# An encoder's token mixer: ones from DRAM, q and k read from a held PSUM bank, and a margin for handing TensorE work of head pairs over

## The chip, the cores and the metric

The kernel runs on one core of a Trainium2 chip. The metric is the device time of one execution in microseconds (us). The engines are TensorE (PE, matmuls; its weight loads are shown as PEld), VectorE (DVE), ScalarE (ACT), GpSimd (POOL) and SyncE (SP, which here only issues DMAs).

## What is computed

Two layers over 256 tokens of width 1024 in float32: half a gated feed-forward step, a mixer of a recurrent branch and an attention branch, and another half feed-forward step. The change touches the attention branch.

```python
h = rms_norm(x, g_mix[l]); z = h @ w_in[l]
q, k, v = three 1024-column parts of z, as 16 heads of 64
f_logit = 16 columns of z + b_forget[l]
qn, kn = rms_norm(q, g_q), rms_norm(k, g_k)            # per head
cum = cumsum(log_sigmoid(f_logit), over time)
s = qn @ kn.T / 8 + cum[query] - cum[key], causal      # per head
o = softmax(s) @ v
y_lru = (gelu(z_lg) * rg_lru(conv(z_lx))) @ w_lru_out[l]
m = sigmoid(gate_A) * y_lru + sigmoid(gate_B) * (o @ w_attn_out[l])
x = x + m @ w_o[l]
```

## The kernel before

**Main matmuls.** Every float32 weight chunk (two row groups of 128 by 512 columns) is loaded by a DMA into `raw`, split into a high part `whi` (ACT, line 325) and a rest `wlo` (DVE, line 334), and used by `visit` in three matmuls per 128 rows (lines 365 to 367). A block of 512 output columns takes four chunks and, for each of the two groups of 128 tokens (`tok`), 24 matmuls into one PSUM bank. There are two x banks, two y banks and four z banks. In the mixer the blocks come in this order: recurrent input, recurrent gate, v, then q and k of heads 0 to 7 (`hf` 0), q and k of heads 8 to 15 (`hf` 1), four gate blocks, and the three output projections.

**Side work.** What is done with a bank is written as generators (chains). The planner `Sched` runs while the program is written, not on the chip. It keeps a modelled time per engine; after every main matmul group `hook` steps the chains that `may` be stepped by that model. So it fixes the order in which each engine's instructions stand, and each engine then works its queue in that order, waiting where data is missing. A chain yields either a modelled time and an engine or another chain that it waits for. `need` forces a chain to its end, whatever the model says.

```python
def may(self, c):
    if c.wait is not None:
        if not c.wait.over:
            return False
        c.ready = self.now
    if c.eng == "p":
        return c.ready <= self.now
```

**q and k.** `ev_qk` scales a bank by `rs(tok)` into `nat` and squares it into `sq` (ACT). `qk_chain` sums the squares per head (line 883), takes the power -1/2 on POOL (line 887), multiplies `nat` by it (line 890), transposes it on PE into a z bank (`quad`, line 449) and scales it into `qk[w, hf]` (w is 0 for q and 1 for k). In that tile 32 partitions hold rows that pick one head's bias (POOL copies from `ident`, line 910) and 32 hold `cum` (`bias_chain`, lines 309 and 312).

**Head pairs.** `pair_chain(j, prev)` handles heads 2j and 2j+1: scores on PE (line 943), mask and minimum on DVE (959), exponentials on ACT (968), reciprocal (973) and scaling, six transposes (449), copies `pt`, and products with V into a y bank that two pairs share (1001). Before the products it yields `prev`, the pair ahead of it. `att_chain` adds the pairs in order, with at most `NLIVE` = 2 at work, and adds `bias_chain` ahead of pairs 0 and 4. Behind the gate blocks `S.need(att)` waits for all pairs. `ot_chain` splits a y bank when its two pairs are done.

Of the kernel before, what the change touches and what calls it, by code (L numbers as in the profile page):

```python
# [15 lines left out]
P = 128  # L16
# [22 lines left out]
SLACK = 2.5  # L39
IDLE = 1.6  # L40
HSTEP = 3.0
LAT = 0.3
LSIG = 2.6
POW = 2.3
# [3 lines left out]


class Chain:  # L50
    def __init__(self, gen, ready, eng, bg):
        self.gen, self.ready, self.eng, self.bg = gen, ready, eng, bg
        self.over = False
        self.wait = None

# [8 lines left out]
class Sched:  # L64
# [25 lines left out]
    def busy(self, eng):  # L90
        return self.t[eng] - self.now

    def add(self, gen, ready=0.0, eng="p", bg=False):
        c = Chain(gen, ready, eng, bg)
        self.chains.append(c)
        return c

# [16 lines left out]
# [3 lines that stand above are left out]
                return False  # L117
            c.ready = self.now
        if c.eng == "p":
            return c.ready <= self.now  # L120
        if c.bg and self.busy(c.eng) > SLACK:
            return False
        return c.ready <= max(self.now, self.t[c.eng]) + 0.05
# [38 lines left out]
def hybrid_encoder_kernel(  # L162
# [15 lines left out]
    tmp_p = ctx.enter_context(tc.tile_pool(name="tmp", bufs=NTMP))  # L178
    att_p = ctx.enter_context(tc.tile_pool(name="att", bufs=NLIVE))
    sm_p = ctx.enter_context(tc.tile_pool(name="sm", bufs=2))  # L180
    ps_x = ctx.enter_context(tc.tile_pool(name="ps_x", bufs=2, space=bass.MemoryType.PSUM))
    ps_y = ctx.enter_context(tc.tile_pool(name="ps_y", bufs=2, space=bass.MemoryType.PSUM))
    ps_z = ctx.enter_context(tc.tile_pool(name="ps_z", bufs=4, space=bass.MemoryType.PSUM))
# [7 lines left out]
    def new(pool, shape, tag, dt=F32):  # L191
        return pool.tile(shape, dt, tag=tag, name=nm(tag))

    nat_ring, z_ring, y_ring, tmp_ring = [], [], [], []

    def new_nat(n=512):
        r = S.claim(nat_ring, NNAT)
        return new(nat_p, [P, n], "nat"), r
# [23 lines left out]
    def free(s):  # L222
        free_slots.append(s[1])
        s[0] = None
# [4 lines left out]
    def bc(ap, n):  # L229

        return ap.unsqueeze(2).to_broadcast([ap.shape[0], ap.shape[1], n])
# [153 lines left out]
    def block(lhs, evac, pool, ncol=512, norm=None, mixed=False):  # L385

        nk = 1024 // ncol
        n = KD // nk
        i0 = take(n)
        accs = {}  # L390
        order = [(tok, i) for tok in range(NT) for i in range(n)]
        if mixed:
            order = [(tok, i) for i in range(n) for tok in range(NT)]
        for tok, i in order:
            if i == 0:
                a, r = pool()
                accs[tok] = a[:, :ncol], r
            acc, r = accs[tok]

            def fin():  # L400
                evac(tok, acc)
                r.free = True

            if norm is not None:
                norm.before(tok, i * nk)
            visit(i0 + i, acc, lhs, i * nk, tok, i == 0, i == n - 1, fin if i == n - 1 else None)
# [139 lines left out]
    def rs(tok):  # L546
        return rstd[:, tok:tok + 1]

    def xbank():
        r = Rec()  # L550
        return bank(ps_x, "x"), r


# [69 lines left out]


    fw = {}

    def load_fw(l):
        r, rr = new_tmp([P, KD, H])
# [34 lines left out]
    def mix(l, nrm):  # L663
# [213 lines left out]
        qk = {}  # L877
        qk_c = {0: [], 1: []}

        def qk_chain(w, hf, tok, nat, sq, dep):  # L880
            yield dep, "d"
            rq = sm_p.tile([P, 8], F32, tag="rq", name=nm("rq"), bufs=4)
            nc.vector.tensor_reduce(out=rq, in_=sq[0].rearrange("p (h d) -> p h d", d=DH), axis=AX.X, op=ALU.add)
            sq[1].free = True
            nc.vector.tensor_scalar(out=rq, in0=rq, scalar1=1.0 / DH, scalar2=EPS, op0=ALU.mult, op1=ALU.add)
            d = S.use("d", dve_c(512) + 0.1)
            nc.gpsimd.tensor_tensor(out=rq, in0=rq, in1=mhalf, op=ALU.pow)
            yield d + POW, "d"
            n3 = nat[0].rearrange("p (h d) -> p h d", d=DH)
            nc.vector.tensor_tensor(out=n3, in0=n3, in1=bc(rq, DH), op=ALU.mult)  # L890
            yield S.use("d", dve_c(512)), "p"
            ps, rz = zbank()
            quad(nat[0], ps)
            nat[1].free = True
            gcol = gqm[:, l:l + 1] if w == 0 else col(R_GK)
            for e in range(2):
                yield S.now, "d"
                b = slice(e * DH, e * DH + DH)
                scale_any(qk[w, hf][0][b, e, :, tok * P:(tok + 1) * P], k4(ps)[b], gcol[b], 512)
            rz.free = True  # L900

        def quarters(w):

            return [(e, slice(r, r + 32), slice(r ^ 32, (r ^ 32) + 32)) for e, r in ((0, 64 + 32 * w), (1, 32 * w))]

        def new_qk(w, hf):
            t = qk[w, hf] = slot([P, 2, KD // 2, T])
            for e, one, _ in quarters(w):
                c0 = one.start + hf * 8 + e
                nc.gpsimd.tensor_copy(t[0][one, e], bc(ident[one, c0:c0 + 7:2], T))  # L910

        def bias_chain(hf):
            for w in range(2):
                for e, _, acc in quarters(w):
                    yield S.now, "d"
                    n = KD // 2
                    copy_any(qk[w, hf][0][acc, e], cum[acc].unsqueeze(1).to_broadcast([32, n, T]), n * T, S.now, True)


        OT = {}  # L920
# [88 lines left out]
        def att_chain():  # L1009
            while not tables[0]:  # L1010
                if lru.over:
                    break
                yield S.now + 0.5, "p"
            yield late[0]
            live, c = [], None
            for j in range(H // 2):
                for c_ in qk_c[j // 4]:
                    yield c_
                if j % 4 == 0:
                    yield S.add(bias_chain(j // 4), S.now, "d")  # L1020
                if len(live) >= NLIVE:
                    yield live.pop(0)
                c = S.add(pair_chain(j, c), S.now, "p", True)
                live.append(c)
                yield S.now + HSTEP, "p"
            for c in live:
                yield c

        att = None
        for hf in range(2):  # L1030
            for w in range(2):
                new_qk(w, hf)

                def ev_qk(tok, acc):
                    nat = new_nat()
                    scale_any(nat[0], acc, rs(tok), 512)
                    sq = new_tmp()
                    nc.scalar.activation(sq[0], acc, AF.Square, scale=rs(tok))
                    dep = S.use("a", act_c(512, 1))
                    c = S.add(qk_chain(w, hf, tok, nat, sq, dep), dep, "d")  # L1040
                    nat[1].user = sq[1].user = c
                    S.step(c)
                    qk_c[hf].append(c)
                block(lhs, ev_qk, xbank)
            if hf == 0:
                att = S.add(att_chain(), S.now, "p", True)

# [93 lines left out]
    def rows_chain():  # L1141
# [4 lines left out]
        for l in range(L):  # L1146
# [6 lines left out]
            S.use("d", 0.3)  # L1153
            rz.free = True
        free(rows_s)
        yield from load_fw(0)

    def program():
# [75 lines left out]
```

## Time and profile before

| | |
|---|---|
| median of 3 runs (lowest to highest) | 1287.18 us (1287.1 to 1287.46) |
| profiled execution: its time, its span | 1288.31 us, 1286.6 us |
| busy share: PE, PEld, DVE, ACT, POOL | 98%, 81%, 64%, 61%, 7% |
| granted TensorE clock, mean | 0.999 of full speed |
| chain that ended last, by engine | PE 90%, DVE 6%, ACT 2%, DMA 2%, issue 1% |

The span is the time from the first to the last instruction in the profile; what lies around it is 1.7 us. A matmul's record lasts longer than the step to the next one, since matmuls are pipelined; so busy shares of PE are upper bounds, and the step from start to start is the pace. The first layer's mixer lies between about 184 and 450 us, the second layer's between about 820 and 1085 us, with the same pattern.

### The profile page before, as it was taken

The numbers are of one execution on the slowest core, as the hardware profiler recorded it, in microseconds if no ns is written. First come the engines' busy times: TensorE is split into PE (matmuls) and PEld (weight loads), VectorE is DVE, ScalarE is ACT, GpSimd is POOL, SyncE is SP. The second block draws the span as 40 slices with busy tenths as digits, with TensorE's granted clock in tenths as the row PEclk, the third lists the DMA queues.
The fourth block names the chain that finished last, engine by engine and source line by source line (L and its number), as shares of the span: only waits on it lengthen the run. The fifth ranks groups of instructions, "written<-read, shape, count | busy, mean of one in ns | idle before, by whom it ended". The sixth has DMA issues, their size and how long they took to land.

```text
span 1286.6 us, 16397 instructions
## 1 busy us (share of the span) xinstructions
PE 1266.1 (98%) x6033; PEld 1047.3 (81%) x6033; DVE 824.5 (64%) x1151; ACT 780.6 (61%) x1064; POOL 84.9 (7%) x85
## 2 busy tenths in 40 slices
PE   8999999999999999999999999999999999999998
PEld 6888888887778888888888888888877788888887
DVE  5655558799765666555475555678987557655553
ACT  6655556777855456555566555558768455555553
POOL 4000001005100000000000000000250000000000
PEclk9999999999999999999999999999999999999999
DMA  8967667365346657666677776664644465687762
GB/s 265 241 203 206 208 167 237 106 197 153 119 134 202 195 184 215 208 207 209 180 209 218 212 213 213 155 213 126 185 145 141 144 200 159 202 235 208 214 196 80
DMA packets 175488, 241.44 MB, mean 188 GB/s; under 512 B 56440, under 2 KB 68912, under 8 KB 175408
## 3 DMA queue, kind: packets, MB, share of 16 engines
q1 hardware_dynamic: 174560, 240.29, 62.5%
q8 instruction: 47, 0.77, 0.2%
q14 instruction: 33, 0.27, 0.1%
q0 software_dynamic: 832, 0.11, 0.1%
q10 hardware_dynamic: 16, 0.00, 0.0%
HBM read 227.78 MB, written 1.05 MB: 178 GB/s over the span
## 4 chain that ended last, share of the span: by engine, by line
PE 90%; DVE 6%; ACT 2%; DMA 2%; issue 1%; SPq 0%; ACTq 0%; DVEq 0%
PE x L365 13%; PE x L366 13%; PE x L367 13%; PE z L366 12%; PE z L367 12%; PE z L365 12%; PE y L367 3%; PE y L365 3%; PE y L366 3%; PE z L449 2%; DVE wlo L334 2%; PE z L943 2%; PE z L771 1%; DMA nat<-tmp 1%; PE y L1001 1%
## 5 line engine op out<-in xcount | busy, mean ns | idle before, releaser
L334 DVE TENSOR_TENSOR wlo<-raw,whi 128x1024 fp32r<-128x1024 f32 x424 | 514.1, 1227 | 226.0 <-ACT whi L325 218.7
L325 ACT CAST whi<-raw 128x1024 fp32r<-128x1024 f32 x424 | 442.1, 1050 | 248.3 <-PE z L367 126.0
L365 PE MATMUL x<-whi,s 128*128 128x512 f32 x832 | 337.2, 405 | 5.3 <-ACT s L470 3.5
L366 PE MATMUL x<-wlo,s 128*128 128x512 f32 x832 | 325.1, 391 | 1.8 <-DVE wlo L334 1.1
L367 PE MATMUL x<-whi,s 128*128 128x512 f32 x832 | 325.2, 391 | 0.1
L365 PE MATMUL z<-whi,s 128*128 128x512 f32 (+1 forms) x752 | 279.7, 372 | 0.0
L367 PE MATMUL z<-whi,s 128*128 128x512 f32 (+1 forms) x752 | 279.4, 371 | 0.0
L366 PE MATMUL z<-wlo,s 128*128 128x512 f32 (+1 forms) x752 | 279.3, 371 | 0.0
L365 PEld LDWEIGHTS x<-whi,s 128*128 128x128 f32 x832 | 156.5, 188 | 39.0 <-ACT s L470 5.8
L367 PEld LDWEIGHTS x<-whi,s 128*128 128x128 f32 x832 | 156.3, 188 | 34.5 <-DVE s L472 1.2
L366 PEld LDWEIGHTS x<-wlo,s 128*128 128x128 f32 x832 | 156.7, 188 | 32.3 <-DVE wlo L334 1.9
L365 PEld LDWEIGHTS z<-whi,s 128*128 128x128 f32 x752 | 141.7, 188 | 24.4
L366 PEld LDWEIGHTS z<-wlo,s 128*128 128x128 f32 x752 | 141.8, 189 | 24.3
L367 PEld LDWEIGHTS z<-whi,s 128*128 128x128 f32 x752 | 141.7, 188 | 24.3
L312 ACT COPY tmp<-nat 128x1024 uint16<-128x1024 uint16 (+1 forms) x76 | 84.1, 1133 | 68.6 <-DMA nat<-tmp 60.7
L603 DVE SCALAR_TENSOR_TENSOR nat<-z,rstd,nat 128x512 f32<-128x512 f32 (+1 forms) x48 | 33.9, 706 | 61.0 <-PE z L367 61.0
L365 PE MATMUL y<-whi,s 128*128 128x512 f32 x176 | 69.1, 393 | 0.0
L367 PE MATMUL y<-whi,s 128*128 128x512 f32 x176 | 68.6, 390 | 0.0
L366 PE MATMUL y<-wlo,s 128*128 128x512 f32 x176 | 68.6, 390 | 0.0
L502 POOL TENSOR_TENSOR rstd<-msum,mhalf 128x1 f32<-128x1 f32 x12 | 11.8, 985 | 805.8 <-DVE msum L500 805.8
L472 DVE TENSOR_TENSOR s<-tmp,s 128x512 fp32r<-128x512 f32 (+1 forms) x72 | 47.2, 656 | 22.6 <-ACT s L470 22.6
L598 ACT ACTIVATE nat<-z,rstd 128x512 f32<-128x512 f32 (+1 forms) x46 | 30.0, 651 | 48.9 <-PE z L367 48.9
(154 smaller groups left out, 919.2 us busy)
## 6 DMA issues: line engine op xcount, KB each, us to landing
raw<-in_w_up_dram SPq DMA_DIRECT2D x176, 512.0 KB, 4.6
raw<-in_w_in_dram SPq DMA_DIRECT2D x112, 512.0 KB, 4.3
raw<-in_w_down_dram SPq DMA_DIRECT2D x88, 512.0 KB, 4.5
raw<-in_w_lru_out_dram SPq DMA_DIRECT2D x16, 512.0 KB, 3.6
raw<-in_w_attn_out_dram SPq DMA_DIRECT2D x16, 512.0 KB, 4.8
raw<-in_w_o_dram SPq DMA_DIRECT2D x16, 512.0 KB, 4.6
tmp<-in_b_gate_dram SPq DMA_DIRECT2D x8, 256.0 KB, 4.3
xn<-in_x_dram SPq DMA_DIRECT2D x4, 256.0 KB, 5.0
```

Source lines behind the costliest of these rows:

```text
L312: nc.scalar.copy(out_, in_)
L325: nc.scalar.copy(hi, raws[i])
L334: nc.vector.tensor_tensor(out=lo, in0=raws.pop(i), in1=f32(hi), op=ALU.subtract)
L365: nc.tensor.matmul(acc, lhsT=lhs(0, k0 + kk)[:, ts], rhs=hi[:, kk, :], start=st, stop=False)
L366: nc.tensor.matmul(acc, lhsT=lhs(0, k0 + kk)[:, ts], rhs=lo[:, kk, :], start=False, stop=False)
L367: nc.tensor.matmul(acc, lhsT=lhs(1, k0 + kk)[:, ts], rhs=hi[:, kk, :], start=False, stop=sp)
L449: nc.tensor.transpose(dst_ps[:, j * P:(j + 1) * P], src[:, j * P:(j + 1) * P], ident)
L472: nc.vector.tensor_tensor(out=lo, in0=t, in1=f32(hi), op=ALU.subtract)
L598: nc.scalar.activation(s[tok][0], acc, AF.Silu, scale=rs(tok))
L603: nc.vector.scalar_tensor_tensor(out=h, in0=acc, scalar=rs(tok), in1=h, op0=ALU.mult, op1=ALU.mult)
L771: nc.tensor.matmul(ps[:, g, :], lhsT=wax[0][:, g, n, :], rhs=xr[0][:, n, :], start=True, stop=True)
L943: nc.tensor.matmul(p_[:, qb * P:qb * P + nk], lhsT=qk[0, hf][0][:, e, jj, qb * P:(qb + 1) * P], rhs=qk[1, hf][0][:, e, jj, :nk], start=Tru ...
```

## The change

The tiles with the rows of ones are made once by ACT (`ones_chain`), written to DRAM, and read from there by DMAs on the POOL queue where POOL copied before. `ev_qk` no longer scales into `nat`: the bank is held (`held`, `r.free`) until `qk_chain` multiplies it by `rs(tok)` and by the per-head factor in one DVE instruction that reads PSUM; k of `hf` 0 goes to the y banks. `Chain` gets a field `late`, 1.5 for pairs and for q and k, by which PE work of such a chain is handed over later than the model has it ready. `bias_chain` ends with a wait for its last copy.

```diff
-    def __init__(self, gen, ready, eng, bg):
-        self.gen, self.ready, self.eng, self.bg = gen, ready, eng, bg
+    def __init__(self, gen, ready, eng, bg, late):
+        self.gen, self.ready, self.eng, self.bg, self.late = gen, ready, eng, bg, late
...
         if c.eng == "p":
-            return c.ready <= self.now
+            return c.ready + c.late <= self.now
...
             def fin():
-                evac(tok, acc)
-                r.free = True
+                held[0] = r
+                r.free = evac(tok, acc) is None
...
     def xbank():
-        r = Rec()
+        r = S.claim(x_ring, 2)
...
+    ones_d = [dram.tile([P, 2, KD // 2, T], F32, name=f"ones_d{hf}") for hf in range(2)]
+    def ones_chain():
+        for hf in range(2):
+            t = slot([P, 2, KD // 2, T])
+            for w in range(2):
+                for e, one, _ in quarters(w):
+                    c0 = one.start + hf * 8 + e
+                    yield S.now, "a"
+                    nc.scalar.copy(t[0][one, e], bc(ident[one, c0:c0 + 7:2], T))
+                    S.use("a", act_c(4 * T))
+            for e in range(2):
+                b = slice((1 - e) * DH, (2 - e) * DH)
+                nc.gpsimd.dma_start(out=ones_d[hf][b, e], in_=t[0][b, e])
+            free(t)
...
             yield d + POW, "d"
-            n3 = nat[0].rearrange("p (h d) -> p h d", d=DH)
-            nc.vector.tensor_tensor(out=n3, in0=n3, in1=bc(rq, DH), op=ALU.mult)
+            nat = new_nat()
+            h3 = lambda t: t.rearrange("p (h d) -> p h d", d=DH)
+            nc.vector.scalar_tensor_tensor(out=h3(nat[0]), in0=h3(acc), scalar=rs(tok), in1=bc(rq, DH), op0=ALU.mult,
+                                           op1=ALU.mult)
+            r.free = True
...
             for e, one, _ in quarters(w):
-                c0 = one.start + hf * 8 + e
-                nc.gpsimd.tensor_copy(t[0][one, e], bc(ident[one, c0:c0 + 7:2], T))
+                nc.gpsimd.dma_start(out=t[0][one, e], in_=ones_d[hf][one, e])
...
-                    copy_any(qk[w, hf][0][acc, e], cum[acc].unsqueeze(1).to_broadcast([32, n, T]), n * T, S.now, True)
+                    end = copy_any(qk[w, hf][0][acc, e], cum[acc].unsqueeze(1).to_broadcast([32, n, T]), n * T, S.now, True)
+            yield end, "p"
...
-                c = S.add(pair_chain(j, c), S.now, "p", True)
+                c = S.add(pair_chain(j, c), S.now, "p", True, LATE)
...
-                    nat = new_nat()
-                    scale_any(nat[0], acc, rs(tok), 512)
+                    r = held[0]
                     sq = new_tmp()
                     nc.scalar.activation(sq[0], acc, AF.Square, scale=rs(tok))
                     dep = S.use("a", act_c(512, 1))
-                    c = S.add(qk_chain(w, hf, tok, nat, sq, dep), dep, "d")
-                    nat[1].user = sq[1].user = c
+                    c = S.add(qk_chain(w, hf, tok, acc, r, sq, dep), dep, "d", False, LATE)
+                    r.user = sq[1].user = c
...
-                block(lhs, ev_qk, xbank)
+                    return c
+                block(lhs, ev_qk, ybank if w > hf else xbank)
```

How the order moves on PE, first layer, inside the third and fourth gate bank of the kernel before (x are main matmuls, z_3226 and z_3229 the scores of pair 6, z_3243 and z_3247 the transposes of pair 5):

```order
L367 MATMUL x_3149<-whi_3099,s_284_1587 128x512
L943 MATMUL z_3226<-s_522_2790,s_490_2649 128x128
L943 MATMUL z_3226<-s_522_2790,s_490_2649 128x256
L943 MATMUL z_3229<-s_522_2790,s_490_2649 128x128
L943 MATMUL z_3229<-s_522_2790,s_490_2649 128x256
L365 MATMUL x_3239<-whi_2925,s_283_1586 128x512
L366 MATMUL x_3239<-wlo_3001,s_283_1586 128x512
L367 MATMUL x_3239<-whi_2925,s_284_1587 128x512
L449 MATMUL z_3243<-ident,pr_3165 128x128 x3
L449 MATMUL z_3247<-ident,pr_3165 128x128 x3
```

The scores of one pair and the transposes of another stand among main matmuls, three or more of them between most such sets. In the changed kernel the last main matmul of the last gate bank (x_3275), on PE in the same layer, is followed by this (y_2987 and y_3329 hold products of pairs 1 and 2, the z_33 banks scores and transposes of pair 3):

```order
L371 MATMUL x_3275<-whi_3216,s_286_1605 128x512
L1025 MATMUL y_2987<-pt_2966,s_413_2269 64x256 x2
L1025 MATMUL y_2987<-pt_2966,s_413_2269 64x128 x2
L1025 MATMUL y_3329<-pt_3108,s_413_2269 64x256 x2
L1025 MATMUL y_3329<-pt_3108,s_413_2269 64x128 x2
L967 MATMUL z_3334<-s_468_2552,s_448_2455 128x128
L967 MATMUL z_3334<-s_468_2552,s_448_2455 128x256
L967 MATMUL z_3337<-s_468_2552,s_448_2455 128x128
L967 MATMUL z_3337<-s_468_2552,s_448_2455 128x256
L453 MATMUL z_3357<-ident,pr_3340 128x128 x3
L453 MATMUL z_3361<-ident,pr_3340 128x128 x3
L1025 MATMUL y_3329<-pt_3365,s_413_2269 64x256 x2
```

Work of pairs that stood among the gate blocks now stands behind them; pairs 3 to 7 follow each other in this way in both layers, up to the first output projection. On ACT, in the first feed-forward step, the kernel before has this (s_119 is a part of the gated activations, nat its next input):

```order
L470 CAST s_119_688<-tmp_861 128x4x128
L325 CAST whi_936<-raw_849 128x1024
L598 ACTIVATE nat_973<-z_939,rstd 128x512
L325 CAST whi_982<-raw_856 128x1024
L325 CAST whi_994<-raw_896 128x1024
```

and the changed kernel, at the same place on ACT, this (s_165 and s_168 are the tiles of ones):

```order
L474 CAST s_119_692<-tmp_865 128x4x128
L644 COPY s_165_937<-ident 32x1024 x4
L644 COPY s_168_949<-ident 32x1024 x4
L657 CAST fw_958<-tmp_956 128x8x16
L329 CAST whi_977<-raw_853 128x1024
L602 ACTIVATE nat_988<-z_942,rstd 128x512
L329 CAST whi_997<-raw_860 128x1024
```

Eight copies now stand ahead of the cast of the next weight chunk.

## Rows read from the trace of the kernel before

**Rows 1.** The page, busy time, share of the span and instructions of each engine.

```profile
PE 1266.1 (98%) x6033; PEld 1047.3 (81%) x6033; DVE 824.5 (64%) x1151; ACT 780.6 (61%) x1064; POOL 84.9 (7%) x85
```

**Rows 2.** Waits, whole span: waiting engine, line <- releaser: us, times, longest.

```profile
PE z L943 <- DVE s L309: 3.5, 2, 1.8
PE z L449 <- ACT pt L312: 2.2, 2, 1.1
```

**Rows 3.** Timeline of PE, first feed-forward step: start, us, instruction, [idle before].

```profile
111.41 0.39 PE L365 MATMUL z<-whi,s 128*128 128x512 f32 x1
...
112.77 0.39 PE L365 MATMUL z<-whi,s 128*128 128x512 f32 x1
```

**Rows 4.** Timeline of PE, gate blocks of the first layer: two sets of scores.

```profile
361.63 1.47 PE L943 MATMUL z<-s,s 128*128 128x128 f32 x8
...
368.08 1.47 PE L943 MATMUL z<-s,s 128*128 128x128 f32 x8
```

**Rows 5.** Chain that ended last, first layer's pairs: start, us, instructions.

```profile
331.54 0.80 PE y L1001 x8
332.34 1.51 PE z L943 x8
```

**Rows 6.** Timelines of DVE and ACT in the first layer's pairs.

```profile
333.24 0.29 DVE L959 CUSTOM_DVE_ANT_0 pr<-z,posm 128x128 f32<-128x128 f32 x1 [0.90 <-PE z L943]
...
371.36 0.41 ACT L968 ACTIVATE pr<-pr,mn 128x128 f32<-128x128 f32 x1
...
373.03 0.19 ACT L968 ACTIVATION_READ_ACCUMULATOR pr<-pr,mn 128x1 f32 x1
...
373.47 1.01 DVE L460 TENSOR_SCALAR pr<-pr,rd 128x128 f32<-128x128 f32 x4
...
364.50 0.56 DVE L309 COPY pt<-z 128x384 f32<-128x384 f32 x1 [0.71 <-PE z L449]
```

**Rows 7.** Timeline of POOL, DVE and PE in the first layer's k block.

```profile
291.60 1.23 DVE L334 TENSOR_TENSOR wlo<-raw,whi 128x1024 fp32r<-128x1024 f32 x1
...
293.24 3.60 POOL L910 COPY s<-ident 32x1024 f32<-32x1024 f32 x2
...
293.88 2.06 DVE L334 TENSOR_TENSOR wlo<-raw,whi 128x1024 fp32r<-128x1024 f32 x1
...
295.86 1.53 DVE L890 TENSOR_TENSOR nat<-nat,rq 128x512 f32<-128x512 f32 x1
...
297.53 0.63 PE L449 MATMUL z<-ident,nat 128*128 128x128 f32 x4 [0.88 <-DVE nat L890]
```

**Rows 8.** Timelines of ACT and DVE: a y bank is split.

```profile
367.25 0.58 ACT L470 CAST s<-y 128x512 fp32r<-128x512 f32 x1
...
368.71 0.69 DVE L472 TENSOR_TENSOR s<-y,s 128x512 fp32r<-128x512 f32 x1
```

**Rows 9.** Timeline of DVE: a gate bank's eviction, two bias copies.

```profile
361.83 0.75 DVE L1059 SCALAR_TENSOR_TENSOR s<-x,rstd,tmp 128x512 f32<-128x512 f32 x1 [0.50 <-PE x L367]
...
348.19 1.38 DVE L309 COPY s<-cum 32x1024 f32<-32x1024 f32 x2
```

**Rows 10.** Windows: stretch, us, busy PE PEld DVE ACT POOL, granted clock, DMA.

```profile
296.00:312.00 16.00, 13.38 (x66) 10.58 (x66) 14.85 (x20) 9.90 (x12) 11.05 (x7) 1.00 0.53 166
1282.00:1285.20 3.20, 0.83 (x4) 0.37 (x2) 0.69 (x1) 0.00 (x0) 0.00 (x0) 1.00 0.22 82
1285.20:1286.60 1.40, 0.00 (x0) 0.00 (x0) 0.00 (x0) 0.00 (x0) 0.00 (x0) 0.51 0.00 0
```

**Rows 11.** Timeline of ACT: a weight cast; two bias copies.

```profile
102.10 1.05 ACT L325 CAST whi<-raw 128x1024 fp32r<-128x1024 f32 x1
...
345.91 2.10 ACT L312 COPY s<-cum 32x1024 f32<-32x1024 f32 x2
```

**Rows 12.** Timelines of ACT and POOL, k of heads 0 to 7: square, power.

```profile
301.15 0.69 ACT L1038 ACTIVATE tmp<-x,rstd 128x512 f32<-128x512 f32 x1 [0.50 <-DVE nat L460]
...
302.85 2.54 POOL L887 TENSOR_TENSOR rq<-rq,mhalf 128x8 f32<-128x8 f32 x1 [2.04 <-ACT whi L325]
```

More of the change, by code (lines that the diff above doesn't have):

```diff
@@ L41 @@
 HSTEP = 3.0
+LATE = 1.5
 LAT = 0.3
@@ L91, in busy, with add @@
         return self.t[eng] - self.now
-    def add(self, gen, ready=0.0, eng="p", bg=False):
-        c = Chain(gen, ready, eng, bg)
+    def add(self, gen, ready=0.0, eng="p", bg=False, late=0.0):
+        c = Chain(gen, ready, eng, bg, late)
         self.chains.append(c)
@@ L180, in hybrid_encoder_kernel @@
     sm_p = ctx.enter_context(tc.tile_pool(name="sm", bufs=2))
+    dram = ctx.enter_context(tc.tile_pool(name="dram", bufs=1, space=bass.MemoryType.DRAM))
     ps_x = ctx.enter_context(tc.tile_pool(name="ps_x", bufs=2, space=bass.MemoryType.PSUM))
@@ L192, in new @@
         return pool.tile(shape, dt, tag=tag, name=nm(tag))
-    nat_ring, z_ring, y_ring, tmp_ring = [], [], [], []
+    nat_ring, z_ring, y_ring, x_ring, tmp_ring = [], [], [], [], []
+    held = [None]
     def new_nat(n=512):
@@ L625, in hybrid_encoder_kernel, with quarters @@
     fw = {}
+    ones_d = [dram.tile([P, 2, KD // 2, T], F32, name=f"ones_d{hf}") for hf in range(2)]
+    def quarters(w):
+        return [(e, slice(r, r + 32), slice(r ^ 32, (r ^ 32) + 32)) for e, r in ((0, 64 + 32 * w), (1, 32 * w))]
+    def ones_chain():
[11 more added lines that the diff above has]
+            free(t)
     def load_fw(l):
@@ L878, in mix, with qk_chain @@
         qk_c = {0: [], 1: []}
-        def qk_chain(w, hf, tok, nat, sq, dep):
+        def qk_chain(w, hf, tok, acc, r, sq, dep):
             yield dep, "d"
@@ L900, in qk_chain @@
             rz.free = True
-        def quarters(w):
-            return [(e, slice(r, r + 32), slice(r ^ 32, (r ^ 32) + 32)) for e, r in ((0, 64 + 32 * w), (1, 32 * w))]
         def new_qk(w, hf):
@@ L908, in new_qk @@
             for e, one, _ in quarters(w):
-                c0 = one.start + hf * 8 + e
-                nc.gpsimd.tensor_copy(t[0][one, e], bc(ident[one, c0:c0 + 7:2], T))
+                nc.gpsimd.dma_start(out=t[0][one, e], in_=ones_d[hf][one, e])
         def bias_chain(hf):
+            end = 0.0
             for w in range(2):
@@ L1155, in rows_chain @@
         free(rows_s)
+        yield from ones_chain()
         yield from load_fw(0)
```

## The prediction

> **What bounds the kernel now.** I read the busy totals first, then the waits, then the order of instructions, then the timeline. TensorE (PE) is at work in 98% of the span [rows 1], and its 512-column matmuls follow each other every 0.227 us: six start-to-start steps take 1.36 us [rows 3]. So time falls only where PE waits and rises only where PE is made to wait; what VectorE (DVE), ScalarE (ACT) and GpSimd (POOL) save by themselves is worth nothing. In the mixer three waits per layer stand out: head-pair scores wait for the bias copy (3.5 us in both layers), pair transposes wait for a bank still being copied out (2.2 us) [rows 2], and the transposes of q wait 0.88 us for `nat` in the first layer [rows 7]. That is 1.75 + 1.1 + 0.88 = 3.7 us a layer, and 4 us with what a matmul's record hides of each. Everything that the change can win in the mixer is about 2 x 4 = 8 us.
>
> **Ones by DMA.** Two POOL copies take 3.60 us; beside them a DVE subtraction takes 2.06 us instead of 1.23 us, and the product on `nat` 1.53 us: that is the 0.88 us wait [rows 7]. Sixteen DMAs replace the sixteen copies, on the same POOL queue as the `pow` steps. Each fills a tile that the first scores read two blocks later; two blocks are 96 matmuls, 21.8 us, so only a landing slower than that costs anything. I count 0 for it and the wait as gone. `ones_chain` adds eight ACT copies of 32x1024 in a row, 1.05 us each by the like copies of `cum` [rows 11], so 8.4 us ahead of the `whi` cast that starts at 102.10 us [rows 11]; PE's first matmul on that chunk is at 112.77 us [rows 3]. The cast now ends near 111.9 us, the subtraction near 113.1 us, and the two evictions and casts queued behind them leave PE late by about 0.6 us, once. Bounds: 0 and 3 us.
>
> **The held bank.** Eight scalings out of PSUM per layer go, and the product on `nat` now reads PSUM. A q or k bank is then free only after square, sum, `pow` and product: from the square's start at 301.15 us to the `pow`'s end at 305.39 us is 4.2 us, and about 0.75 us for the product [rows 9, 12], so 5 us. With k of the first half on the y banks, the tightest return is one bank per layer, 24 matmuls and a transpose group later: 5.4 + 0.45 us. I take 0; with the queues as full as in this stage it could be 0 to 2 us a layer.
>
> **The margin.** Here the sum is decided. `may` sets a chain that waits for another chain to `ready = now` at every look, and then asks for `ready + late <= now`. With `late = 1.5` that is never true, even when the other chain is over; only the forced step in `need` goes past it. Every pair but the first waits for its predecessor (`yield prev`), so pair 1 is stuck before its output product, pair 2 too, `NLIVE = 2` lets no further pair start, and all waits for `S.need(att)` behind the last gate matmul. The order shows just that: after the last gate matmul come the products of pairs 1 and 2, and then pairs 3 to 7 each complete, scores, transposes, products, with no main matmul between them, in both layers. PE's queue is in order, so pair n+1's scores stand behind pair n's products.
>
> What such a pair costs: scores start to the first DVE pass 0.90 us (332.34 to 333.24) [rows 5, 6]; 0.32 us to the first exponential (one pass and a handoff); four exponentials 1.86 us (371.36 to 373.22); reciprocal until the first scaling 0.25 us; three scalings on DVE 0.80 us (four take 1.01) [rows 6]; handoff to PE 0.14 us and the last transposes 0.5 us (a group of four takes 0.63) [rows 7]; handoff and copy out 0.04 + 0.56 us [rows 6]; handoff 0.14 us; products until the next scores 0.80 us [rows 5]. Sum 6.3 us. In the kernel before, a pair costs PE only its own work: from 361.63 to 368.08 us [rows 4] lie one set of scores, one of transposes, one of products and 15 main matmuls; 6.45 - 15 x 0.227 = 3.05 us. The difference, 3.25 us, is paid by five pairs: 16.3 us a layer.
>
> Two more items. Products of pairs 4 and 6 go to a y bank that must first be split, and the cast (0.58 us) and subtraction (0.69 us) [rows 8] stand in the queues behind that pair's own copies: about 0.8 us of it shows, twice. And DVE enters the stage late: last gate eviction 0.75 us, one `wlo` 1.23 us, three bias copies of 0.69 us [rows 7, 9] are 4.0 us, while the scores of pair 3 could be read 1.6 + 0.9 us after the last matmul: 1.5 us. Per layer: 16.3 + 1.6 + 1.5 - 4 = +15.4 us; two layers and the copies at the start: +31 us. On the profiled run (1288.31 us, 1286.6 of it span) that is 1319; on the median of 1287.18 it is **1318 us, if TensorE's clock holds**.
>
> **The clock.** It holds in every stretch of the trace before, also where PE waits the 1.75 us: 296 to 312 us is granted 1.00, with 13.38 us of 16 at work. It falls once: from 1282.0 us PE is at work for its last 0.83 us, and from 1285.2 us on the granted clock is 0.51, the lower level of 1.2 GHz [rows 10], 2.4 us after the last matmul. In the new stage PE is idle for some 2.3 us between scores and transposes of every pair, and at work in under half of the time. That is nearer to the row in which the clock fell than to the one in which it held, so I take it to fall in part of the stage. At the lower level PE's sets last twice as long: of a pair, about +1.0 us on the way to the last exponential (scores take 1.3 us at the upper level), +0.3 us in the transposes, +0.7 us in the products: +2 us. With half of the five pairs at the lower level: +5 us a layer, +10 in all: **1328 us**.
>
> The Trainium skill (TensorE: Matmul & The Clock Gate, section "HAM oscillation — how this bites in real kernels") says that short bursts of matmuls between waits can throw the engine back to half rate, and make each burst start cold; no stage of the trace before has such bursts, so no row here tests it. By that rule, taken for every burst, the sum would be the third case below; with no fall at all it would be the 1318 us above.
>
> **Rivals.**
> 1. The clock holds: 1318 us. For it: 1.75 us of waiting did no harm. Against it: the fall 2.4 us after the last matmul.
> 2. The clock falls for all five pairs and for the first matmuls after them: 10 us a layer, and up to 1.2 us each until it rises: 1318 + 20 + 2 = 1341 us. The Trainium skill's page named above would lead here.
> 3. Faster. The tail costs no more than the pairs cost in line, because the engines overlap one pair's scores with the last one's softmax: then only the removed waits count, 1287.2 - 8 + 0.6 = 1280 us. It would need a pair to pass in 3.05 us; break-even with the items above lies at about 3.2 us a pair. Against it: four exponentials alone take 1.86 us, and the scores stand behind the products in PE's own queue.
> 4. The pairs as in the first case, and new waits at the held banks of 2 us a layer, plus 3 us at the start: 1324 us, inside the range. That the margin never lets work pass is itself the case in which the change does not do what it says; my forecast rests on it.
>
> **How the numbers follow.** Forecast (clock lower in part) 0.45, rival 1 0.30, rival 2 0.12, rival 4 0.08, faster 0.03, no change 0.02. A pair known to 0.6 us is 6 us over ten pairs, so 1318 reaches down to 1311; 1341 reaches up to 1342. The range is 1311 to 1342. A measurement of this kernel can tell 0.2% (2.6 us) from no change; faster by more 0.03, within 0.02, slower 0.95.
>
> **What would show it.** Right: in each mixer a stretch of 35 to 43 us behind the gates in which no main matmul stands, PE is at work less than half of the time, five sets of scores lie 6 to 8.5 us apart, and the granted clock is below 1.00 in places; ahead of it PE runs without the waits of rows 2; ACT has eight 32x1024 copies near 102 us. Wrong: sets of scores under 4 us apart, main matmuls among them, or PE waits of over 3 us a layer for `nat` or for a bank in the q and k blocks.

## The result and the profile after

The changed kernel takes 1342.0 us (median of 4 runs, 1339.98 to 1346.51); the kernel before, run beside it, 1287.32 us. The ratio is 1.0431, 95% interval 1.0418 to 1.0444: 55 us slower. Direction and mechanism were forecast, but 1328 us was 14 us too low: the time lies at the very top of the range, beside rival 2 (1341 us). So what follows asks which terms were too small.

The page of the changed kernel, answering to [rows 1] (span; busy time, share and instructions; TensorE's busy tenths and granted clock in 40 slices):

```profile
span 1344.8 us, 16412 instructions
...
PE 1295.4 (96%) x6033; PEld 1066.3 (79%) x6033; DVE 826.3 (61%) x1159; ACT 778.2 (58%) x1048; POOL 74.5 (6%) x89
...
PE   8999999999977999999999999999999689999998
...
PEclk9999999999986999999999999999999789999999
```

There is a dent in each of the two mixers, in TensorE's work and in its clock. The waits of the whole span (engine, line <- releaser: us in total, times, longest) answer to [rows 2]:

```profile
PE z L453 <- DVE pr L464: 27.5, 10, 5.6
PE y L1025 <- DVE s L476: 5.4, 4, 1.5
PE x L369 <- DVE nat L915: 3.7, 4, 1.0
PE x L369 <- ACT tmp L1061: 1.6, 2, 0.8
```

The same view for VectorE, one row:

```profile
DVE s L1083 <- DMA tmp<-in_b_gate_dram: 22.8, 4, 6.3
```

Both rows of [rows 2] are gone. In their place pair transposes wait for the scaled probabilities ten times, which is pairs 3 to 7 in two layers; products wait four times for a y bank to be split; main matmuls of the last k block and of the first gate block wait six times for a bank that still holds q or k (`nat` L915 is the product that frees a held bank, L1061 the square that reads it); and VectorE waits up to 6.3 us for a gate bias. TensorE's timeline shows where the serial stretch of the first layer begins, and then one pair of it (start, us, instructions, [idle before]):

```profile
380.66 0.39 PE L371 MATMUL x<-whi,s 128*128 128x512 f32 x1
380.98 1.52 PE L1025 MATMUL y<-pt,s 128*64 128x256 f32 x16
382.43 1.58 PE L967 MATMUL z<-s,s 128*128 128x128 f32 x8
389.64 1.51 PE L453 MATMUL z<-ident,pr 128*128 128x128 f32 x6 [5.63 <-DVE pr L464]
...
393.27 2.75 PE L967 MATMUL z<-s,s 128*128 128x128 f32 x8
398.06 0.94 PE L453 MATMUL z<-ident,pr 128*128 128x128 f32 x6 [2.04 <-DVE pr L464]
400.45 1.55 PE L1025 MATMUL y<-pt,s 128*64 128x256 f32 x8 [1.45 <-DVE s L476]
401.93 2.93 PE L967 MATMUL z<-s,s 128*128 128x128 f32 x8
```

After the last gate matmul at 380.66 us come the products of pairs 1 and 2, then scores, transposes and products of one pair after another, and no main matmul until 427.70 us. A set of scores that lasted 1.47 us in [rows 4] lasts 2.75 and 2.93 us here, and 8.66 us lie between two sets. The windows (stretch; us; busy PE, PEld, DVE, ACT, POOL; granted clock; DMA share; GB/s) say why, and answer to [rows 10]:

```profile
360.00:380.00 20.00, 20.00 (x90) 16.54 (x89) 8.36 (x10) 6.99 (x8) 0.00 (x0) 1.00 0.70 221
380.00:388.00 8.00, 4.00 (x29) 2.66 (x27) 7.91 (x16) 3.78 (x8) 0.00 (x0) 1.00 0.58 192
388.00:396.00 8.00, 6.36 (x22) 4.32 (x22) 2.19 (x9) 2.55 (x10) 0.00 (x0) 0.57 0.04 14
396.00:404.00 8.00, 4.51 (x22) 3.32 (x22) 3.27 (x13) 2.69 (x10) 0.00 (x0) 0.70 0.00 0
404.00:412.00 8.00, 5.96 (x22) 3.72 (x21) 2.45 (x11) 2.80 (x10) 0.00 (x0) 0.50 0.00 0
```

From 388 us on most of the stretch has the lower level, 1.2 GHz. Not all of it: six transposes of a pair take 1.51 us at 389.64 us and 0.94 us at 398.06 us. In the second layer the windows between 1052 and 1092 us have 0.58 to 0.78. DMA moves next to nothing there; I take it that the weights that fit are already in.

To see in which part of the program time goes, I took the start of the same main matmuls (5,280 in all, in TensorE's order) from each trace, so each row but for its median is one execution. Between number 422 and 528 lie the eight copies of ones; 1161 to 1584 holds q, k, pairs and gates of the first layer; 3168 to 4224 those of the second; 1584 to 3168 is what lies between. All in us:

| kernel | median | 422 to 528 | 1161 to 1584 | 1584 to 3168 | 3168 to 4224 |
|---|---|---|---|---|---|
| before | 1287.3 | 24.03 | 129.20 | 356.25 | 280.02 |
| changed | 1342.0 | 24.64 | 158.21 | 356.30 | 306.01 |
| LATE = 0 | 1280.15 | 24.76 | 124.40 | 356.24 | 275.09 |
| margin alone | 1339.1 | 24.03 | 155.27 | 356.15 | 305.93 |
| TensorE kept at work | 1325.75 | 24.29 | 147.42 | 355.69 | 299.63 |
| gate biases by POOL's queue | 1338.05 | 24.82 | 153.75 | 356.53 | 305.74 |
| ones by POOL, LATE = 0 | 1277.85 | 24.03 | 124.50 | 356.27 | 274.53 |
| no held bank, LATE = 0 | 1278.7 | 24.89 | 124.48 | 356.03 | 274.57 |
| no end wait, LATE = 0 | 1287.7 | 24.75 | 129.14 | 355.85 | 279.88 |
| end wait alone | 1280.99 | 24.03 | 125.69 | 356.47 | 276.43 |
| margin on q, k alone | 1286.62 | 24.71 | 129.00 | 356.03 | 279.75 |

The change costs 29.0 and 26.0 us in the two mixers and 0.6 us at the copies. What lies between the mixers is the same to 0.1 us, so nothing is given back there. (Another 2.3 us in the profiled run, which at 1346.51 us was above the median, lie at a norm: from 184 to 188 us the clock is granted 0.57, where the kernel before has 1.00.)

### The profile page after: what moved, and what is told of

The parts are those of the page before. It is cut to its first block, busy times and chain, and to the rows that moved or that the text cites. A ratio compares the mean times of both kernels' runs of the same rounds, so it can differ in the third digit from the quotient of the medians.

```text
span 1344.8 us, 16412 instructions
## 1 busy us (share of the span) xinstructions
PE 1295.4 (96%) x6033; PEld 1066.3 (79%) x6033; DVE 826.3 (61%) x1159; ACT 778.2 (58%) x1048; POOL 74.5 (6%) x89
## 4 chain that ended last, share of the span: by engine, by line
PE 89%; DVE 4%; DMA 3%; ACT 2%; issue 1%; SPq 0%; DVEq 0%; ACTq 0%
PE x L369 12%; PE x L371 12%; PE x L370 12%; PE z L370 11%; PE z L371 11%; PE z L369 11%; PE y L369 4%; PE y L371 4%; PE y L370 4%; PE z L453 3%; PE z L967 2%; DMA tmp<-in_b_gate_dram 2%; DVE wlo L338 1%; PE y L1025 1%; PE z L795 1%; ACT pr L992 1%
## 5 line engine op out<-in xcount | busy, mean ns | idle before, releaser
L369 PE MATMUL x<-whi,s 128*128 128x512 f32 x800 | 322.4, 403 | 9.4 <-DVE nat L915 3.7
L370 PE MATMUL x<-wlo,s 128*128 128x512 f32 x800 | 313.4, 392 | 1.4 <-DVE mhalf L1153 0.8
L371 PE MATMUL x<-whi,s 128*128 128x512 f32 x800 | 313.5, 392 | 0.0
L369 PEld LDWEIGHTS x<-whi,s 128*128 128x128 f32 x800 | 151.2, 189 | 44.0 <-ACT s L474 5.0
L371 PEld LDWEIGHTS x<-whi,s 128*128 128x128 f32 x800 | 150.9, 189 | 33.1 <-DVE s L476 0.6
L370 PEld LDWEIGHTS x<-wlo,s 128*128 128x128 f32 x800 | 151.5, 189 | 31.7 <-DVE wlo L338 1.5
L369 PE MATMUL y<-whi,s 128*128 128x512 f32 x208 | 82.0, 394 | 0.0
L371 PE MATMUL y<-whi,s 128*128 128x512 f32 x208 | 81.1, 390 | 0.0
L370 PE MATMUL y<-wlo,s 128*128 128x512 f32 x208 | 81.0, 389 | 0.0
L474 ACT CAST s<-tmp 128x512 fp32r<-128x512 f32 (+1 forms) x72 | 42.6, 592 | 29.6 <-DVE tmp L486 29.0
```

Of the source, the lines that this page charges most:

```text
L369: nc.tensor.matmul(acc, lhsT=lhs(0, k0 + kk)[:, ts], rhs=hi[:, kk, :], start=st, stop=False)
L370: nc.tensor.matmul(acc, lhsT=lhs(0, k0 + kk)[:, ts], rhs=lo[:, kk, :], start=False, stop=False)
L371: nc.tensor.matmul(acc, lhsT=lhs(1, k0 + kk)[:, ts], rhs=hi[:, kk, :], start=False, stop=sp)
L474: nc.scalar.copy(hi, t)
```

## The experiments

**The margin taken away, and the margin alone.** Theory: the margin makes nearly all of the loss. Rival: the transfers of ones or the held banks do. First the changed kernel with

```diff
-LATE = 1.5
+LATE = 0.0
```

> The changed kernel with one number changed: LATE is 0 instead of 1.5, so a chain that waits for another may go as soon as that one is over. Ones by DMA, the held bank and the end wait of the bias copies all stay. Theory (nearly all of the 55 us comes from the margin, which leaves pairs 3 to 7 serial behind the gates): the stretch behind the gates is gone, in-line pairs as before; 8 us won at the waits of before, some 5 us given to the new waits at the held banks, 0.6 at the start: 1280 to 1287 us. Rival A (the held banks or the transfers of ones carry a large part): 1300 us or more, with the tail gone. Rival B (the tail has another cause than the margin): 1335 to 1345 us, tail still there.

Measured: 1280.15 us, ratio to before 0.9938 (0.9925 to 0.995), no serial stretch, and no wait for a held bank either, although the banks are held here too. Then the kernel before with the margin and nothing else:

```diff
-            return c.ready <= self.now
+            return c.ready + c.late <= self.now
-                c = S.add(pair_chain(j, c), S.now, "p", True)
+                c = S.add(pair_chain(j, c), S.now, "p", True, LATE)
-                    c = S.add(qk_chain(w, hf, tok, nat, sq, dep), dep, "d")
+                    c = S.add(qk_chain(w, hf, tok, nat, sq, dep), dep, "d", False, LATE)
```

> The kernel before with the margin alone (LATE = 1.5 on the pairs and on the chains of q and k); POOL copies of ones, separate scaling of q and k and the x banks stay as they were. Theory: the same stretch of five serial pairs behind the gates in both layers, 1338 to 1350 us (1342 plus the waits that only the other parts take away, less those that they bring). Rival A: 1287 to 1315 us, since the rest of the 55 us would belong to the other parts.

Measured: 1339.1 us, ratio 1.0395 (1.0376 to 1.0415). Its wait `PE z L450 <- DVE pr L461: 27.6, 10, 6.1` is that of the changed kernel. The theory stands from both sides: the margin costs 52 to 62 us, and the rest of the change wins 7.

**Two ways to mend the test.** If the fault is that a chain that waits for another never counts as late enough, one line in `may` must do. First the margin left off for such chains:

```diff
-            c.ready = self.now
+            c.ready = self.now - c.late
```

> The changed kernel with one line of `may` changed: when the chain waited for is over, ready is set to now - late, so that the margin holds for times that are worked out and not for the end of another chain. Theory: the pairs stand between main matmuls again, no serial stretch: 1278 to 1287 us; next to the kernel with LATE = 0 it shows what a margin that lets work pass is worth, 0 to 4 us either way. Rival B: 1335 us or more.

Measured: 1282.31 us, ratio 0.9964 (0.9951 to 0.9976). Then the margin counted once from the look that finds the other chain over:

```diff
                 return False
+            c.wait = None
             c.ready = self.now
```

> The changed kernel with one line of `may` added: the waited-for chain is forgotten once it is over, so ready is set once and the margin of 1.5 us is then counted from there. By the order of instructions one pair per layer is left behind the gates instead of five. Theory (the cost goes by the number of serial pairs, plus the lead-in once per layer): one pair of 3 to 4 us and a lead-in of 1.5 to 6 us per layer, so 9 to 20 us above the kernel of the third run: 1290 to 1305 us. Rival C (the cost is that of the lead-in and of the clock's fall, whatever the number of pairs): over 1315 us.

Measured: 1297.27 us, ratio 1.0072 (1.0059 to 1.0084). One pair per layer is left behind the gates, and the kernel is 15 us slower than the one with none. TensorE's timeline in the first layer:

```profile
392.76 1.58 PE L968 MATMUL z<-s,s 128*128 128x128 f32 x8
396.60 0.94 PE L454 MATMUL z<-ident,pr 128*128 128x128 f32 x6 [2.26 <-DVE pr L465]
397.78 1.27 PE L1026 MATMUL y<-pt,s 128*64 128x256 f32 x8 [0.24 <-ACT pt L317]
```

Here the scores still last 1.58 us, and the clock stays at 1.00. In the second layer, where no main matmul stands for 11.0 us (9.3 in the first), the clock does fall near the end of this one pair. Two windows:

```profile
1032.00:1036.00 4.00, 1.75 (x11) 1.26 (x9) 2.00 (x12) 2.26 (x9) 0.00 (x0) 1.00 0.28 101
1036.00:1040.00 4.00, 3.76 (x17) 2.45 (x18) 1.15 (x4) 1.40 (x3) 0.00 (x0) 0.63 0.00 0
```

So the cost grows with the number of serial pairs, and one pair can be enough for a short fall of the clock.

**The price of the clock.** The changed kernel, with transposes of the identity into a bank that nobody reads in the places where TensorE waits:

```diff
+            if j >= 3:
+                if j == 3:
+                    spare[0] = bank(ps_x, "x")
+                for _ in range(44 if j == 3 else 14):
+                    nc.tensor.transpose(spare[0][:, :P], ident, ident)
...
+            if j >= 3:
+                for _ in range(3):
+                    nc.tensor.transpose(spare[0][:, :P], ident, ident)
             yield end, "p"
             if prev is not None:
```

> The changed kernel with TensorE kept at work in the serial stretch: behind the scores of each pair from 3 on, 14 transposes of the identity (44 behind pair 3) into an x bank that nobody reads, and 3 more behind the pair's transposes. No result depends on them. Theory (the serial pairs cost 8.6 us instead of 6.3 because the granted clock falls to its lower level there): granted clock 1.00 through the stretch, pairs 6.2 to 7 us apart, 15 to 25 us less than the changed kernel: 1317 to 1327 us. Rival A (the pairs are long because of DVE and ACT, the clock does not matter to them): 1338 to 1346 us. Rival B (the added transposes lie in the way): over 1346 us.

Measured: 1325.75 us, ratio 1.0293 (1.0279 to 1.0307): 16.3 us less than the changed kernel, although TensorE does more. Its windows, three in the first layer and two in the second:

```profile
388.00:396.00 8.00, 6.14 (x47) 5.08 (x46) 3.92 (x17) 3.29 (x12) 0.00 (x0) 1.00 0.01 2
396.00:404.00 8.00, 7.25 (x55) 5.86 (x52) 3.74 (x19) 4.53 (x18) 0.00 (x0) 1.00 0.00 1
404.00:412.00 8.00, 5.43 (x41) 4.42 (x42) 4.39 (x18) 3.67 (x13) 0.00 (x0) 1.00 0.00 0
...
1054.00:1062.00 8.00, 6.14 (x47) 4.89 (x45) 3.53 (x14) 3.23 (x11) 0.00 (x0) 0.95 0.01 2
1062.00:1070.00 8.00, 7.49 (x46) 5.84 (x42) 3.53 (x14) 3.81 (x12) 0.00 (x0) 0.83 0.00 0
```

And TensorE's timeline over two pairs of the first layer (L975 and L1023 are the added transposes):

```profile
394.65 1.58 PE L968 MATMUL z<-s,s 128*128 128x128 f32 x8
396.07 1.69 PE L975 MATMUL x<-ident 128*128 128x128 f32 x14
398.49 0.94 PE L453 MATMUL z<-ident,pr 128*128 128x128 f32 x6 [0.73 <-DVE pr L464]
...
400.88 1.58 PE L968 MATMUL z<-s,s 128*128 128x128 f32 x8
402.29 1.69 PE L975 MATMUL x<-ident 128*128 128x128 f32 x14
404.71 0.94 PE L453 MATMUL z<-ident,pr 128*128 128x128 f32 x6 [0.73 <-DVE pr L464]
405.49 0.49 PE L1023 MATMUL x<-ident 128*128 128x128 f32 x3
407.11 0.87 PE L1034 MATMUL y<-pt,s 128*64 128x256 f32 x8 [1.13 <-DVE s L476]
407.91 1.36 PE L968 MATMUL z<-s,s 128*128 128x128 f32 x7
```

In the first layer the clock is 1.00 throughout; the pairs are 6.23 us apart (394.65 to 400.88), and 7.03 us where a y bank must first be split (to 407.91). In the second it still falls once, near the end of the stretch: the last two pairs take 7.50 and 7.14 us there, where the first layer's take 7.03 and 6.22, 1.4 us more. So the clock's share of the 62 us between this change with and without its margin is 16.3 us and a little more.

**The late start of the stretch.** Before the first serial pair the changed kernel's VectorE does this:

```profile
379.93 0.75 DVE L1083 SCALAR_TENSOR_TENSOR s<-x,rstd,tmp 128x512 f32<-128x512 f32 x1 [6.28 <-DMA tmp<-in_b_gate_dram]
380.60 2.35 DVE L338 TENSOR_TENSOR wlo<-raw,whi 128x1024 fp32r<-128x1024 f32 x2
382.86 0.75 DVE L1083 SCALAR_TENSOR_TENSOR s<-x,rstd,tmp 128x512 f32<-128x512 f32 x1
383.52 1.22 DVE L338 TENSOR_TENSOR wlo<-raw,whi 128x1024 fp32r<-128x1024 f32 x1
384.77 2.08 DVE L313 COPY s<-cum 32x1024 f32<-32x1024 f32 x3
386.78 0.27 DVE L983 CUSTOM_DVE_ANT_0 pr<-z,posm 128x128 f32<-128x128 f32 x1
```

The last gate bias is issued on SP's queue behind weight loads, at 372.96 us, 0.7 us before VectorE first wants it; the weight loads in turn wait for their buffers. The test moves these loads to POOL's queue:

```diff
-                nc.sync.dma_start(out=bg, in_=b_gate[l, c0:c0 + 512].partition_broadcast(P))
+                nc.gpsimd.dma_start(out=bg, in_=b_gate[l, c0:c0 + 512].partition_broadcast(P))
```

> The changed kernel with one word changed: the four loads of the gate biases per layer are issued from POOL's queue instead of SP's, where the last of them stands behind weight loads and lands 6.3 us after DVE first wants it. Theory (the first serial pair starts late because DVE does its last gate evictions late, and this load is why): the first gap of each stretch shrinks from 5.6 and 5.2 us to 2.5 to 3 us, 1334 to 1338 us. Rival (DVE is late for its other work, or the load lands late from either queue): 1340 to 1344 us.

Measured: 1338.05 us, 4.0 us less than the changed kernel; ratio 1.0387 (1.0371 to 1.0403). VectorE no longer waits for the load, and the first gap is shorter:

```profile
384.77 1.51 PE L453 MATMUL z<-ident,pr 128*128 128x128 f32 x6 [3.86 <-DVE pr L464]
```

It was 5.63 us in the first layer and 5.16 in the second, and is 3.86 in both, not the 2.5 to 3 expected: the last eviction, one subtraction and three bias copies on VectorE remain. So the load is a part of the late start, not all of it. Nor are the 4.0 us its price alone: in the table the first mixer is 4.5 us shorter for a gap that is 1.8 us shorter, and the second 0.3 us for 1.3. Where the lower level lies differs from execution to execution: here the windows from 380 to 396 us have 0.80 and 0.93, in the changed kernel 1.00 and 0.57.

**What each of the other parts is worth.** All with LATE = 0, so that pairs pass. With the POOL copies of ones back:

```diff
-                nc.gpsimd.dma_start(out=t[0][one, e], in_=ones_d[hf][one, e])
+                c0 = one.start + hf * 8 + e
+                nc.gpsimd.tensor_copy(t[0][one, e], bc(ident[one, c0:c0 + 7:2], T))
...
-        yield from ones_chain()
```

> The kernel with LATE = 0 (1280 us) with the ones written by sixteen POOL copies again, without ones_chain and the tiles in DRAM; the held bank and the end wait of the bias copies stay. Theory (the transfers took away the slow stretch on DVE beside POOL's copies, which cost PE 0.9 us in a layer): 1280 to 1283 us. Rival A (the transfers cost more than the copies): 1276 to 1279 us. Rival B (most of the 7 us won come from the transfers): 1285 us or more.

Measured: 1277.85 us, ratio 0.9921 (0.9908 to 0.9935), in the range of rival A. The theory fell: beside the held bank the transfers win nothing. The wait for `nat` is 1.5 us in two layers with the transfers and with the copies, and the copies at the start cost TensorE 0.7 us (24.03 to 24.76 in the table). With q and k scaled twice again, on x banks alone:

```diff
-                    r = held[0]
+                    nat = new_nat()
+                    scale_any(nat[0], acc, rs(tok), 512)
...
-            nat = new_nat()
-            h3 = lambda t: t.rearrange("p (h d) -> p h d", d=DH)
-            nc.vector.scalar_tensor_tensor(out=h3(nat[0]), in0=h3(acc), scalar=rs(tok), in1=bc(rq, DH), op0=ALU.mult,
-                                           op1=ALU.mult)
-            r.free = True
+            n3 = nat[0].rearrange("p (h d) -> p h d", d=DH)
+            nc.vector.tensor_tensor(out=n3, in0=n3, in1=bc(rq, DH), op=ALU.mult)
```

> The kernel with LATE = 0 (1280 us) with q and k scaled out of PSUM into nat at once and nat scaled again, as before, all four blocks on the x banks; ones by transfer and the end wait of the bias copies stay. Theory (the held bank moves work from engine to engine and takes no wait away by itself): 1278 to 1282 us. Rival A (its eight scalings less per layer are what made room: it carries the gain): 1284 to 1288 us.

Measured: 1278.7 us, ratio 0.9932 (0.9919 to 0.9944): beside the transfers the held bank wins nothing either. No wait for `nat` is left in this kernel. What is left is the line that ends `bias_chain`. Taken out:

```diff
-            yield end, "p"
```

> The kernel with LATE = 0 (1280 us) without the one line at the end of `bias_chain` that tells the planner when the last bias copy is done; ones by transfer and the held bank stay. Theory (that line, which lets the scores of pairs 0 and 4 stand behind matmuls until the copies are there, carries the gain, since neither the transfers nor the held bank showed any): the wait of the scores for the bias copies is back at 1.7 us per layer, 1283 to 1288 us. Rival A (the gain is in the parts together, or comes with any new order): 1278 to 1281 us.

Measured: 1287.7 us, ratio 1.0003 (0.9995 to 1.0012). And alone on the kernel before:

```diff
+            end = 0.0
...
-                    copy_any(qk[w, hf][0][acc, e], cum[acc].unsqueeze(1).to_broadcast([32, n, T]), n * T, S.now, True)
+                    end = copy_any(qk[w, hf][0][acc, e], cum[acc].unsqueeze(1).to_broadcast([32, n, T]), n * T, S.now, True)
+            yield end, "p"
```

> The kernel before with two lines changed: `bias_chain` ends in a wait for its last copy, as in the changed kernel. No ones by transfer, no held bank, no margin. Theory (this line carries the gain): 1277 to 1281 us, no wait of scores for the bias copies. Rival A: 1284 to 1288 us, because the wait for `nat` beside POOL's copies and the wait for `pt` stay.

Measured: 1280.99 us, ratio 0.9948 (0.9934 to 0.9961). So this line carries most of the gain, 6 of the 7 us, and without it there is none. In the waits of the kernel without it the wait of the scores (L965) is back:

```profile
PE z L965 <- ACT whi L329: 3.4, 2, 1.7
```

The row names a cast on ScalarE as the releaser; place, number and size are those of the first row of [rows 2]. With the line alone neither row of [rows 2] is left, and of the mixer's own steps only the transposes of q and k still wait:

```profile
PE z L449 <- DVE nat L890: 2.2, 4, 0.9
```

This row also says more of the two other parts. What the kernel without the held bank has and this one has not are the transfers, and the wait is gone there; what the one with the POOL copies has is the held bank, and the wait is 1.5 us. In the table each of the two is 1.2 and 1.9 us shorter than this kernel in the two mixers, and with both parts it is no more (1.3 and 1.3 us). So in these executions transfers and held bank each win some 3 us where the other is missing. The medians (1278.7, 1277.85, 1280.99 us) go the same way, but their intervals overlap or all but touch, so the times alone do not show it.

**The margin on q and k alone.** The changed kernel without `LATE` on the pairs:

```diff
-                c = S.add(pair_chain(j, c), S.now, "p", True, LATE)
+                c = S.add(pair_chain(j, c), S.now, "p", True)
```

> The changed kernel with the margin of 1.5 us on the chains of q and k alone, none on the pairs. Theory (the chains of q and k wait for times, not for another chain, so the margin lets them pass): no serial stretch, 1279 to 1284 us. Rival: their margin holds something too, and 5 us or more of the 62 us between the changed kernel and the one with LATE = 0 stay: 1286 us or more.

Measured: 1286.62 us, ratio 0.9991 (0.9983 to 1.0). The theory fell and the rival held: no serial stretch, but 6.5 us more than with LATE = 0 stay. The waits for a held bank are back:

```profile
PE x L369 <- DVE nat L915: 5.8, 4, 2.1
```

And the longest of them in the timelines of ScalarE, VectorE, POOL and TensorE, with the window behind it:

```profile
322.79 0.69 ACT L1061 ACTIVATE tmp<-x,rstd 128x512 f32<-128x512 f32 x1
...
327.02 0.68 DVE L907 TENSOR_REDUCE rq<-tmp 128x8 f32<-128x512 f32 x1
...
328.05 1.64 POOL L911 TENSOR_TENSOR rq<-rq,mhalf 128x8 f32<-128x8 f32 x1 [11.65 <-DVE rq L909]
...
328.41 2.35 DVE L338 TENSOR_TENSOR wlo<-raw,whi 128x1024 fp32r<-128x1024 f32 x2
330.68 0.75 DVE L915 SCALAR_TENSOR_TENSOR nat<-x,rstd,rq 128x512 f32<-128x512 f32 x1
...
331.48 0.50 PE L369 MATMUL x<-whi,s 128*128 128x512 f32 x1 [2.07 <-DVE nat L915]
...
332.00:336.00 4.00, 4.00 (x14) 3.30 (x14) 1.43 (x7) 0.00 (x0) 1.64 (x1) 0.57 0.76 271
```

The square is done at 323.48 us, but the sum on VectorE comes only at 327.02. The power is done at 329.69 us (328.05 + 1.64), but the product that frees the held bank stands behind two weight subtractions in VectorE's queue until 330.68: about 1.0 of the 2.07 us. Behind this wait the granted clock falls, to 0.57 in the next window, and in the second layer likewise. Waits (2.9 us a layer) and clock (an estimate from the window: 4 us at 0.57, 1.7 us) make up about the 4.6 us by which each mixer is longer than with LATE = 0. With LATE = 0 the order is another one and the list of waits has no such row. Why this margin, which acts on TensorE's steps alone, puts the product so late in VectorE's order was not followed further.

No kernel beats that with the POOL copies and LATE = 0 (1277.85 us); the intervals of the four at 1278 to 1281 us overlap or all but touch, so they are not ranked here.

## Why the prediction came out 14 us too low: its mechanism held, three of its sizes did not

**The bound** was read rightly: between the mixers nothing moved, and in the profiled execution 55 us are TensorE waiting or clocked down inside them.

**The margin** does what the prediction reads out of `may`: pairs 3 to 7 serial behind the gates in both layers, ten waits, no main matmul for 47.0 and 45.2 us from the start of the last one (expected 35 to 43), sets of scores 7.9 to 8.7 us apart, and 10.9 and 10.4 us behind the first one (expected 6 to 8.5). A pair was costed at 6.3 us at the upper level: measured 6.23 where the clock was kept at 1.00. The split of a y bank was put at 0.8 us: 7.03 - 6.23 = 0.80. Both terms were built from [rows 4 to 8], and they stand.

**Removed waits**, 4 us a layer: 4.8 and 4.9 us with LATE = 0 (table). The size was about right. A cause was named for the wait for `nat` alone, the transfers; which part removes the two waits of [rows 2] was left open. It is the end wait of the bias copies: without it none of the gain comes, and alone it wins 3.5 and 3.6 us. The wait for `pt`, too, goes with the new order.

**Ones.** The start was put at 0.6 us: 24.64 - 24.03 = 0.61. ScalarE's row answers to [rows 11], with 8.48 us where 8.4 was counted:

```profile
102.34 8.48 ACT L644 COPY s<-ident 32x1024 f32<-32x1024 f32 x8
```

The prediction's own times would end the cast at 111.55 us (102.10 + 8.4 + 1.05), not at 111.9, so the agreement of the 0.6 us is in part luck. The transfers land in 4.3 us (median), well inside the 21.8 us that they had. That they remove the wait for `nat` is borne out where q and k are scaled twice (2.2 us with the copies, none with the transfers), not beside the held bank (1.5 us either way).

**The steps that failed** are three sizes, the clock's the largest.

1. *Held bank*: "I take 0", with 0 to 2 us a layer as bounds. Measured in the changed kernel 5.3 us in two layers (3.7 + 1.6 in the waits), and in the last experiment 5.8. With LATE = 0 there is no such wait, so it takes the margin on q and k as well, which the prediction priced for pairs alone. The return time of 5 us was counted with sum and product on VectorE at once; left out was the queue ahead of them, as the last experiment shows it.
2. *Lead-in*: 1.5 us a layer. Without the wait for the gate bias the first gap is 3.86 us, where later ones are 2.0 to 2.3: 1.6 to 1.8 us, as costed. The wait adds 1.8 and 1.3 us (5.63 and 5.16). VectorE waits for these loads in the kernel before as well (11.3 us in two waits), and TensorE's list of waits there has nothing of it: main matmuls cover it. What else that cover hid was not asked.
3. *Clock*: "half of the five pairs at the lower level: +5 us a layer". The price of 2 us per pair was near: between sets in the first layer lie 8.66, 8.59 and 8.58 us, where the kernel with TensorE at work has 7.03, 6.23 and 7.03: 1.85 us a pair on average. In the second layer they are 8.43, 7.92 and 8.63 us, 1.56 us a pair more than at 1.00. So all pairs paid it, at least in part, and not half of them: 16.3 us by the experiment, not 10. One fall and one hold were in [rows 10], and half was a guess between them. Rival 2, with 0.12 (the "third case below" of the prediction), read the clock better. That its 1341 us is so close is luck: it put 22 us on the clock, more than was measured, and nothing on the first two sizes. (As printed, its sum 1318 + 20 + 2 gives 1340.)

The sum closes to within 1 us, as an estimate. With TensorE kept at work the time is 1325.75 us, not 1318: held banks 5.2 us (3.6 + 1.6 in that run); the two stretches 37.24 and 38.82 us instead of 36.4 (1.8 for the products of pairs 1 and 2, 1.5, five times 6.3, 1.6), 3.3 us, of which 1.4 us are the clock's one fall there; less 1.7 us of waits won beyond the 8 (4.8 + 4.9, taken over from LATE = 0). That is 6.8 of the 7.75 us. The clock brings 16.3 instead of 10: 6.3 us. Together 13.1 of the 14 us. That "PE is at work less than half of the time" did not hold in the windows (4.0 to 6.4 of 8 us): at the lower level its instructions last longer.

The sentence of the Trainium skill cited in the prediction (TensorE: Matmul & The Clock Gate, section "HAM oscillation — how this bites in real kernels"), that short bursts of matmuls between waits can throw the engine back to half rate, agrees with the windows of the changed kernel (0.50 to 0.70 between 388 and 412 us), where the trace before had no such stretch. That each burst then starts cold is not so here: the six transposes at 398.06 us, behind a wait of 2.04 us, last 0.94 us, as they do at 1.00.

## What to carry to other kernels

Ask of a condition in a planner that compares a time with the present whether it can come true at all when the time is set anew at every look: here one such line cost 52 to 62 us and hid a gain of 7. When work falls out of the cover of other work, list everything that the same cover hid (here a load in a queue of weights), and price the clock for every pair of such a stretch rather than for half of them. Try the parts of a change alone and left out one at a time: of four parts, one line carried most of the gain, two seemed to win nothing beside each other, and the fourth lost eight times as much as all of them won.

## What was not expected of the hardware

Seventeen transposes per pair (47 for the first) that nobody reads kept the clock at 1.00 through the first layer's stretch, also in a window in which TensorE's records fill 5.43 of 8 us; without them it was granted 0.50 in a window with 5.96 of 8 us, and the kernel with more work was 16.3 us faster. With the margin on q and k alone, one wait of 2.07 us was followed by a window at 0.57, in which TensorE was at work all the time. And a 256 KB load behind weight loads on its queue kept VectorE waiting 6.3 us, which another queue took away.
